# Last two expert groups summed expert by expert, and another order of the first loads, in a decoder layer with 32 experts

## The chip, the cores and the metric

One Trainium2 chip, one of its cores. The metric is the device time of one execution in microseconds (us), the median of three runs.

## The reference

One decoder layer on 256 tokens of width 1024, in float32. The part that the change touches is the input projection of the attention and the mixture of experts.

```
h    = rms_norm(x) * norm1_g                      # 256 x 1024
proj = h @ w_in                                   # 1024 x 3072: q, k, v of two head groups
...                                               # attention of both groups, output projection, x = x + ...
t    = rms_norm(x) * norm2_g
g    = argmax(t @ router_group)                   # 1 of 4 groups
e    = top 2 of the group's 8 experts             # weights: p_group * softmax of the two
y[token] += weight * ((silu(t @ w_gate[e]) * (t @ w_up[e])) @ w_down[e])
out  = x + y                                      # hidden width of an expert: 256, 32 experts
```

## The kernel before, in words

**Weights.** All weights pass through SBUF in units of 1 MB: 12 of `w_in`, 4 of `w_out`, then gate, up and down of the 32 experts, in the order in which they are used (gate e, up e, down e−2). A ring of 16 buffers and a few more tiles hold them; `fill` (L120) issues every load on SyncE's queue (SP) as soon as the list `used` says that the buffer's earlier unit is consumed in program order, and the transfer itself waits on the chip until the reader is done. `unit` (L145) calls it.

**Start.** TensorE warms up on zeros (`keep_warm`, L161). x comes twice: transposed (`xt`, into qT and kT, which are free at that time) for the projection, and in rows (x2, L406) for the residual and for the scale of the RMS norm. `x_split` (L197) makes of each 128-wide slice k of the transposed x a rounded half `xh` (ScalarE) and a remainder `xl` (VectorE); `stage` (L239) does the same with 128 rows of a weight unit (`hi` on ScalarE, `lo` on VectorE, two of them on POOL). Four buffers of each are in rotation. A product is then three matmuls (xh·hi, xl·hi, xh·lo), for each of the two token halves c. The projection runs over six column groups ng of 512 columns (q, k, v, twice), each with eight slices k, two to a step b. The two accumulators of a group (`pps`) are both PSUM buffers of their tag, so the next group begins when they are copied out by `post_qk` (L264). That copy multiplies with `rstd`, which `x_norm` (L205) makes from x2 by two squares with a sum (L209), a logarithm and an exponential (L153, L154) and some small VectorE work.

**Experts.** Eight groups g of four experts, 32 slots each. `prep` (L607) makes a group's selection matrices Pm and Ps and gathers its tokens (L615). Per expert: `gate` (L662), `folded` of the expert before (L672), `up` (L668), and `down` (L696) of the one before that; the loop is at L881. A group's results gather in `oG`, 32 rows an expert, by four copies an expert (L707, L709); `weighted` (L633) makes the weighted, transposed selection pT, and `combine` (L723) adds the whole group to the four accumulators y with 8 matmuls (16 instructions) two experts later. The last group goes another way: `weighted_last` (L620) makes a pT for each of its experts with the selection repeated four times, at expert 30; `down` leaves its result in the four row blocks of one 128 x 256 tile, two copies (`moved`, L711); and `spread` (L715) adds one expert with 8 matmuls (16 instructions) on 32 rows each. `residual` (L731) adds x through the identity. `last` (L736) does the second half of expert 31's down product in two halves of the columns, each with its copy, its spread, and its stores. `overflow` (L755), after expert 28, is a branch that all engines take part in; it is not taken with these inputs.

The order of each engine's instructions is made when the program is built, by a scheduler that works with priorities; in the expert loop `pe` (L647) keeps TensorE in program order.

Of the kernel before, what the change touches and what calls it, by code (L numbers as in the profile page):

```python
# [20 lines left out]
P = 128  # L21
S = 256
# [29 lines left out]
def hybrid_layer_kernel(ctx: ExitStack, tc: tile.TileContext, x, xt, w_in, w_out, w_gate, w_up, w_down, smalls, relb, out):  # L52
# [49 lines left out]
    units[0] = (*units[0][:2], 2)  # L102
# [17 lines left out]
    def fill(i, limit=len(units)):  # L120
        while len(tiles) < limit:
# [49 lines left out]
    with ExitStack() as att:  # L171
# [67 lines left out]
        def stage(u, k):  # L239
# [4 lines left out]
            (nc.gpsimd if u * 4 + k in (0,3,) else nc.vector).tensor_tensor(lo, raw, hi.bitcast(F32), op=ALU.subtract)  # L244
# [195 lines left out]
        for ng, what in enumerate("qkvqkv"):  # L440
            g = ng // 3
            pps = new_pp()
            for b in range(4):
# [7 lines left out]
                for c in range(NC):  # L451
                    products(hl, c, b * 2, b == 0, b == 3, pps[c])
# [137 lines left out]
    CROSS = [(j, c) for c in range(NC) for j in range(4)]  # L590
# [29 lines left out]
    def weighted_last(st):  # L620
        t = pools["late"].tile([P, 2048], F32, name="oL", tag="late")
        st["o"], st["pT"] = t[:, :D].rearrange("p (i n) -> p i n", i=G), t[:, D:].rearrange("p (i t) -> p i t", i=G)
        for i in range(G):
            pt = ps.tile([P, 512], F32, name="ptr", tag="tr")
            for c in range(NC):
                q = st["P"][c][1].rearrange("p (j s) -> p j s", j=G)
                e = st["g"] * G + i
                nc.vector.tensor_scalar(q, st["P"][c][0][:, i : i + 1, :].broadcast_to([P, G, CAP]),
                                        W[:, c, e : e + 1], None, op0=ALU.mult)
                pe(nc.tensor.transpose(pt[:, c * P : (c + 1) * P], q.rearrange("p j s -> p (j s)"), ident))  # L630
            nc.scalar.activation(st["pT"][:, i, :], pt[:, :S], AF.Copy)

    def weighted(st):  # L633
        g = st["g"]
        if g == E // G - 1:
            return weighted_last(st)
# [59 lines left out]
    def down(e, st, hT, low):  # L696
# [4 lines left out]
        if st["g"] == E // G - 1:  # L701
            moved(st, i, pd, slice(0, P))
            return
# [7 lines left out]
    def moved(st, i, pd, rows):  # L711
# [277 lines left out]
```

## Time and profile before

| what | value |
|---|---|
| median of 3 runs | 344.23 us (343.37 to 344.47) |
| the profiled execution: its time, its span | 344.96 us, 343.2 us |
| TensorE busy, share of the span | 314.5 us, 92% |
| VectorE, ScalarE, POOL busy | 194.3, 139.9, 17.3 us |
| read from HBM | 121.64 MB, 358 GB/s over the span |

The span is shorter than the time of the execution by what lies around the first and the last instruction. Busy time of TensorE holds matmuls that wait in its pipeline, so a busy fortieth doesn't say that it runs at its peak; what waits for what is in the views below. DMA issues stand as "SPq" and "ACTq", weight loads as "PEld".

### The profile page before, as it was taken

Reading aid. Unit: us, or ns where it says so; the run is one execution under the profiler, and the core shown is the slowest. Engines: PE = TensorE matmul, PEld = TensorE weight load, DVE = VectorE, ACT = ScalarE, POOL = GpSimd, SP = SyncE. Lnnn points to the kernel's source line nnn. Section 1 sums busy time; section 2 is a strip of 40 time slices with the busy share of each in tenths; the row PEclk is TensorE's granted clock in tenths of the full one; section 3 lists DMA queues with packets and bytes.
Section 4 is the critical chain, followed back from the end, with each engine's and each line's share of the span. In section 5 each row is a group of like instructions: output and inputs, shape, how many; then the busy total and the mean of one; then the engine's idle time right before and its main releaser. Section 6 shows DMA issues by size and latency. Waiting matters only on the chain. (4 is left out here: it accounts for less than half of the span.)

```text
span 343.2 us, 7327 instructions
## 1 busy us (share of the span) xinstructions
PE 314.5 (92%) x2801; PEld 217.4 (63%) x2801; DVE 194.3 (57%) x599; ACT 139.9 (41%) x364; POOL 17.3 (5%) x25
## 2 busy tenths in 40 slices
PE   6999999999999999999999999998489669968893
PEld 2758877788777797576666766566257326625461
DVE  1867858869998658665463654736224522532502
ACT  4876667968886443423232232321112211211302
POOL 1100001000110140000000000000000000040000
PEclk9899999999999999999999999999989978989997
DMA  6999999999635888899999999999999999999903
GB/s 197 403 385 317 389 387 402 413 411 409 209 99 210 319 355 320 303 423 418 416 416 415 415 421 418 413 421 413 416 418 416 418 415 420 416 411 420 362 10 122
DMA packets 29496, 123.20 MB, mean 359 GB/s; under 512 B 2295, under 2 KB 3364, under 8 KB 21268
## 3 DMA queue, kind: packets, MB, share of 16 engines
q1 hardware_dynamic: 28868, 121.17, 89.1%
q0 software_dynamic: 304, 1.02, 1.0%
q8 instruction: 23, 0.38, 0.4%
q10 hardware_dynamic: 288, 0.52, 0.4%
q14 instruction: 13, 0.11, 0.1%
HBM read 121.64 MB, written 1.07 MB: 358 GB/s over the span
## 5 line engine op out<-in xcount | busy, mean ns | idle before, releaser
L658 PE MATMUL pgu<-u,xe 128*32 128x256 f32 x976 | 67.4, 395 | 10.1 <-ACT oG L707 4.8
L254 PE MATMUL pp<-hi,xh 128*128 128x512 f32 (+1 forms) x132 | 53.3, 405 | 2.6 <-ACT hi L243 2.6
L254 PE MATMUL pp<-lo,xh 128*128 128x512 f32 (+1 forms) x132 | 52.1, 399 | 0.3 <-POOL lo L244 0.2
L254 PE MATMUL pp<-hi,xl 128*128 128x512 f32 (+1 forms) x132 | 51.9, 393 | 0.0
L707 ACT ACTIVATE oG<-pd 32x256 f32<-32x256 f32 x56 | 21.0, 374 | 75.0 <-PE pd L693 61.4
L658 PEld LDWEIGHTS pgu<-u,xe 128*32 128x32 f32 x976 | 29.5, 111 | 34.6 <-ACT oG L707 8.6
L244 DVE TENSOR_TENSOR lo<-u,hi 128x512 fp32r<-128x512 f32 x62 | 43.1, 714 | 13.0 <-ACT hi L243 12.7
L243 ACT ACTIVATE hi<-u 128x512 fp32r<-128x512 f32 x64 | 38.9, 626 | 18.3 <-PE pp L254 12.6
L709 DVE COPY oG<-pd 32x256 f32<-32x256 f32 x56 | 23.7, 423 | 38.7 <-ACT oG L707 36.8
L693 PE MATMUL pd<-u,hT 128*32 128x256 f32 x496 | 34.9, 394 | 6.6 <-DMA u<-in_w_down_dram 6.6
L254 PEld LDWEIGHTS pp<-hi,xh 128*128 128x128 f32 x132 | 25.1, 190 | 9.6 <-ACT hi L243 4.0
L254 PEld LDWEIGHTS pp<-lo,xh 128*128 128x128 f32 x132 | 25.3, 192 | 7.4 <-issue 1.0
L254 PEld LDWEIGHTS pp<-hi,xl 128*128 128x128 f32 x132 | 25.2, 191 | 4.6
L670 DVE COPY u<-pgu 128x256 f32<-128x256 f32 x30 | 12.7, 422 | 26.7 <-PE pgu L658 23.6
L615 PEld LDWEIGHTS pg<-Ps,x2q 128*128 128x128 f32 x224 | 25.5, 192 | 2.9 <-DVE gu L678 2.9
L693 PEld LDWEIGHTS pd<-u,hT 128*32 128x32 f32 x496 | 14.5, 112 | 20.0 <-DVE u L670 7.5
L615 PE MATMUL pg<-Ps,x2q 128*128 128x128 f32 x224 | 26.9, 278 | 0.0
L728 PE MATMUL y<-oG,pT 128*128 128x256 f32 x112 | 26.4, 391 | 0.0
L728 PEld LDWEIGHTS y<-oG,pT 128*128 128x128 f32 x112 | 21.8, 200 | 2.8
L678 DVE TENSOR_REDUCE gu<-ptr 128x64 f32<-128x256 f32 x32 | 13.6, 425 | 14.5 <-PE ptr L675 13.8
L675 PEld LDWEIGHTS ptr<-sm,u 128*128 128x128 f32 x120 | 13.4, 147 | 13.1 <-issue 9.9
L675 PE MATMUL ptr<-sm,u 128*128 128x128 f32 x120 | 21.0, 301 | 0.0
(166 smaller groups left out, 342.0 us busy)
## 6 DMA issues: line engine op xcount, KB each, us to landing
u<-in_w_up_dram SPq DMA_DIRECT2D x31, 1024.0 KB, 19.9
u<-in_w_gate_dram SPq DMA_DIRECT2D x30, 1024.0 KB, 19.9
u<-in_w_down_dram SPq DMA_DIRECT2D x30, 1024.0 KB, 19.9
u<-in_w_in_dram SPq DMA_DIRECT2D x11, 1024.0 KB, 12.0
u<-in_w_out_dram SPq DMA_DIRECT2D x4, 1024.0 KB, 14.6
x<-in_w_gate_dram SPq DMA_DIRECT2D x2, 1024.0 KB, 9.0
u<-in_w_in_dram SPq DMA_DIRECT2D x2, 512.0 KB, 6.0
x<-in_x_dram SPq DMA_DIRECT2D x2, 512.0 KB, 10.9
```

Of the source, the lines that this page charges most:

```text
L243: nc.scalar.activation(hi, raw, AF.Copy)
L244: (nc.gpsimd if u * 4 + k in (0,3,) else nc.vector).tensor_tensor(lo, raw, hi.bitcast(F32), op=ALU.subtract)
L254: yield lambda a=a, w=w, kk=kk, i=i: nc.tensor.matmul(pp, a, w[:, cols], start=first and kk == 0 and i == 0, stop=last and kk == len(hls) ...
L615: pe(nc.tensor.matmul(pg[:, j * P : (j + 1) * P], x2q[:, c, q4 * 4 + j, :], st["P"][c][1], start=c == 0, stop=c == NC - 1))
L658: pe(nc.tensor.matmul(pg[q * CAP : (q + 1) * CAP, :HID], st["xe"][:, k, j0 : j0 + CAP], wv[:, k, :], start=r == 0, stop=r == KC // ROWS_Q ...
L670: nc.vector.tensor_copy(t[:, HID : 2 * HID], pg[:, :HID])
L675: pe(nc.tensor.transpose(pt[:, j * P : (j + 1) * P], t[:, j * P : (j + 1) * P], ident))
L678: nc.vector.tensor_reduce(gu[:, :2], parts[:, :2], axis=AX.X, op=ALU.add)
L693: pe(nc.tensor.matmul(pd[j * 32 : (j + 1) * 32, :256], hT[:, c, :], dv[:, c, j * 256 : (j + 1) * 256], start=c == 0, stop=c == 1, tile_pos ...
L707: nc.scalar.activation(dst, pd[j * 32 : (j + 1) * 32, :256], AF.Copy)
L709: nc.vector.tensor_copy(dst, pd[j * 32 : (j + 1) * 32, :256])
L728: pe(nc.tensor.matmul(y[j][:, c * 256 : c * 256 + 256], st["pT"][:, c * P : (c + 1) * P], st["o"][:, j * 256 : (j + 1) * 256], start=st["g ...
```

## The change

- The groups 6 and 7 (`APART` is 6) are both summed expert by expert. `weighted_last` is split: `repeated` writes the repeated selection on VectorE, `weighted_last` transposes it and copies it out. For group 6 one expert at a time (24 to 27), for group 7 the experts 28 and 29 at expert 28's turn, 30 and 31 at expert 29's. Every expert's `spread` stands one expert behind its `down`. `combine` is left out for group 6.
- The tiles for these two groups and the copy of x (`res`) take buffers of the ring (`spare`); the copy of x on POOL stands at expert 28, and the residual is added in two pieces, at expert 30 and after 31.
- The last expert's second half goes in one wave: 8 matmul instructions, two copies, one spread, eight copies out, four stores.
- At the start, unit 0 comes in three parts: slice 0 and slice 1 on ScalarE's queue, slices 2 and 3 on SP's. The first slices of the transposed x go ahead on SP, unit 2 goes ahead of x in rows. The table of the activation functions is loaded behind ScalarE's two issues. One of the two remainders on POOL goes to VectorE.
- In the first column group the matmuls run slice by slice with both token halves in each slice, where it was step by step with one half after the other.

```diff
-    nc.scalar.preload_act_table_set("natural_log_exp_and_others")
     head = A_COLS["gq"][0]
-    nc.sync.dma_start(sm[:, :head], smalls[:, :head])
...
-    units[0] = (*units[0][:2], 2)
+    units[0] = (*units[0][:2], 3)
...
                 if j == 0:
-                    ks = slice(q * k // parts, (q + 1) * k // parts)
-                    nc.sync.dma_start(tv[:, ks], src[:, ks])
-                    xt_load(2, 4) if q == 0 else xt_load(4, 8)
+                    ks = slice(*((0, 1), (1, 2), (2, 4))[q])
+                    (nc.sync if q == 2 else nc.scalar).dma_start(tv[:, ks], src[:, ks])
+                    if q == 2:
+                        xt_load(4, 8)
...
-            (nc.gpsimd if u * 4 + k in (0,3,) else nc.vector).tensor_tensor(lo, raw, hi.bitcast(F32), op=ALU.subtract)
+            (nc.gpsimd if u * 4 + k == 3 else nc.vector).tensor_tensor(lo, raw, hi.bitcast(F32), op=ALU.subtract)
...
         keep_warm(11, "av")
+        nc.sync.dma_start(sm[:, :head], smalls[:, :head])
         xt_load(0, 2)
+        xt_load(2, 4)
         unit(0)
+        nc.scalar.preload_act_table_set("natural_log_exp_and_others")
+        early["units"] = 3
+        fill(0, 3)
         for c in range(NC):
             nc.sync.dma_start(x2[:, c, :], x[c * P : (c + 1) * P, :])
...
-                for c in range(NC):
-                    products(hl, c, b * 2, b == 0, b == 3, pps[c])
+                if ng == 0:
+                    for kk in range(2):
+                        for c in range(NC):
+                            products(hl[kk : kk + 1], c, b * 2 + kk, b + kk == 0, b + kk == 4, pps[c])
+                else:
+                    for c in range(NC):
+                        products(hl, c, b * 2, b == 0, b == 3, pps[c])
...
+    APART = E // G - 2
+    def spare(name):
+        used["ring"].append(len(units))
+        return ring.tile([P, 2048], F32, name=name, tag="ring")
+    def last_group(st):
+        t = spare("oL")
...
+    def repeated(st, i):
+        e = st["g"] * G + i
+        for c in range(NC):
+            q = st["P"][c][1].rearrange("p (j s) -> p j s", j=G)
+            nc.vector.tensor_scalar(q, st["P"][c][0][:, i : i + 1, :].broadcast_to([P, G, CAP]),
+                                    W[:, c, e : e + 1], None, op0=ALU.mult)
+    def weighted_last(st, i):
+        pt = ps.tile([P, 512], F32, name="ptr", tag="tr")
+        for c in range(NC):
+            pe(nc.tensor.transpose(pt[:, c * P : (c + 1) * P], st["P"][c][1], ident))
+        nc.scalar.activation(st["pT"][:, i, :], pt[:, :S], AF.Copy)
...
-        if st["g"] == E // G - 1:
-            moved(st, i, pd, slice(0, P))
+        if st["g"] >= APART:
+            moved(st, i, pd)
...
+    def last(st, hT, dv, pd, res):
         for nh in range(2):
             down_product(hT, dv, pd, (1,), (2 * nh, 2 * nh + 1))
+        moved(st, G - 1, pd)
+        spread(st, G - 1)
+        for c in range(NC):
+            for j in range(4):
+                dst = res[:, c, j * 256 : (j + 1) * 256]
+                if j < 2:
+                    nc.scalar.activation(dst, y[j][:, c * 256 : c * 256 + 256], AF.Copy)
+                else:
+                    nc.vector.tensor_copy(dst, y[j][:, c * 256 : c * 256 + 256])
+            for nh, eng in enumerate((nc.scalar, nc.sync)):
...
         if i == 0:
             before, st = old, nxt
+            if g >= APART:
+                last_group(st)
         t = gate(e, st)
         queue.append((e - 1, old, folded(old_t)))
-        if i == 2 and g > 0:
+        apart = () if g < APART else (i,) if g == APART else ((0, 1), (2, 3), (), ())[i]
+        if apart:
+            repeated(st, apart[0])
+        if i == 2 and 0 < g <= APART:
             combine(before)
         up(e, st, t)
+        for k, j in enumerate(apart):
+            if k:
+                repeated(st, j)
+            weighted_last(st, j)
...
+        if done:
+            spread(*done.pop())
         if e == E - 1:
             hT = folded(t)
         if e > 1:
-            down(*queue.pop(0), place[e][0])
+            e2, st2, hT2 = queue.pop(0)
+            down(e2, st2, hT2, place[e][0])
+            if st2["g"] >= APART:
+                done.append((st2, e2 % G))
         if e == OVER_E:
             overflow()
-        if e == E - 1:
-            rt_ = ring.tile([P, 2048], F32, name="res", tag="ring")
-            res = rt_.rearrange("p (c n) -> p c n", c=NC)
+            res = spare("res").rearrange("p (c n) -> p c n", c=NC)
...
+        if e == E - 2:
+            residual(0, res)
+    residual(1, res)
     down(*queue.pop(0), place[E - 1][0])
...
+    spread(*done.pop())
+    dv = unit(place[E - 1][2]).rearrange("p (c n) -> p c n", c=2)
+    pd = ps.tile([P, 512], F32, name="pd", tag="tr")
+    down_product(hT, dv, pd, (0,), range(4))
+    spread(st, 2)
+    warmed(2, "pp")
+    last(st, hT, dv, pd, res)
```

What the scheduler makes of it, at three places. ScalarE behind the halves of unit 1 (u_124), before: the two squares of x (sq,ss) and the scale's logarithms and exponentials (ry) stand ahead of every half (hi) of unit 2 (u_129).

```order
L243 ACTIVATE hi<-u_124 128x512 x4
L209 ACTIVATE sq,ss<-x_64 128x1024 x2
L153 ACTIVATE ry<-rv 128x1
L154 ACTIVATE ry<-ry 128x1
L153 ACTIVATE ry<-rv 128x1
L154 ACTIVATE ry<-ry 128x1
L270 ACTIVATE qk<-pp,rstd 128x512
L276 ACTIVATE sq<-qk 128x512
L243 ACTIVATE hi<-u_129 128x512 x2
```

The same place in the changed kernel (unit 2 is u_127 there):

```order
L242 ACTIVATE hi<-u_124 128x512 x4
L242 ACTIVATE hi<-u_127 128x512 x3
L208 ACTIVATE sq,ss<-x_64 128x1024
L242 ACTIVATE hi<-u_127 128x512
L152 ACTIVATE ry<-rv 128x1
L208 ACTIVATE sq,ss<-x_64 128x1024
L153 ACTIVATE ry<-ry 128x1
L152 ACTIVATE ry<-rv 128x1
L153 ACTIVATE ry<-ry 128x1
L269 ACTIVATE qk<-pp,rstd 128x512
```

All four halves of unit 2 moved ahead of the end of the scale's chain, the fourth to between the two squares.

TensorE from expert 30's gate to expert 28's down, before: behind the fold (ptr<-sm,u) the sum of group 6 (y<-oG,pT), behind the up product eight weighted transposes (ptr<-sm,Ps).

```order
L658 MATMUL pgu<-u_3100,xe 32x256 x8
L675 MATMUL ptr<-sm,u_3042 128x128 x4
L728 MATMUL y<-oG,pT 128x256 x8
L658 MATMUL pgu<-u_3102,xe 32x256 x8
L630 MATMUL ptr<-sm,Ps 128x128 x8
L693 MATMUL pd<-u_3177,hT 32x256 x8
```

The same in the changed kernel:

```order
L673 MATMUL pgu<-u_3101,xe 32x256 x8
L690 MATMUL ptr<-sm,u_3043 128x128 x4
L673 MATMUL pgu<-u_3103,xe 32x256 x8
L733 MATMUL y<-oL 128x256 x8
L708 MATMUL pd<-u_3181,hT 32x256 x8
L748 MATMUL y<-res,sm 128x256 x4
```

The group's sum and the transposes went out; a spread of one expert (27) and half of the residual came in.

TensorE from expert 30's down product to the end, before (pd<-u_3282 is expert 31's):

```order
L693 MATMUL pd<-u_3280,hT 32x256 x8
L733 MATMUL y<-res,sm 128x256 x8
L718 MATMUL y<-oL 128x256 x8
L693 MATMUL pd<-u_3282,hT 32x256 x4
L688 LDWEIGHTS zeros
L688 MATMUL warm<-zeros 128x512
L688 LDWEIGHTS zeros
L688 MATMUL warm<-zeros 128x512
L693 MATMUL pd<-u_3282,hT 32x256 x2
L718 MATMUL y<-oL 128x256 x4
L693 MATMUL pd<-u_3282,hT 32x256 x2
L718 MATMUL y<-oL 128x256 x4
```

The same in the changed kernel (expert 31's is pd<-u_3346):

```order
L708 MATMUL pd<-u_3296,hT 32x256 x8
L733 MATMUL y<-oL 128x256 x8
L708 MATMUL pd<-u_3346,hT 32x256 x4
L733 MATMUL y<-oL 128x256 x8
L703 LDWEIGHTS zeros
L703 MATMUL warm<-zeros 128x512
L703 LDWEIGHTS zeros
L703 MATMUL warm<-zeros 128x512
L708 MATMUL pd<-u_3346,hT 32x256 x4
L733 MATMUL y<-oL 128x256 x8
```

The residual stands ahead of these rows now, and the last expert's two halves are one.

## Rows read from the trace of the kernel before

**Rows 1.** The page, its first line and the row of its second part that gives the memory traffic in 40 equal slices of the span (8.58 us each), in GB/s.

```profile
span 343.2 us, 7327 instructions
GB/s 197 403 385 317 389 387 402 413 411 409 209 99 210 319 355 320 303 423 418 416 416 415 415 421 418 413 421 413 416 418 416 418 415 420 416 411 420 362 10 122
```

**Rows 2.** Who the queue SP waited for before it could issue a load, from 137 to 150 us (first row) and from 180 to 240 us (second): line waited at, releaser, us in total, times, longest.

```profile
SPq L138 <- PE pl L875: 7.9, 1, 7.9
...
SPq L138 <- DMA u<-in_w_gate_dram: 16.5, 8, 2.2
```

**Rows 3.** Who TensorE waited for, from 0 to 150 us; the same columns.

```profile
PE pp L254 <- ACT hi L243: 2.6, 2, 1.9
...
PE pp L856 <- DVE gi L546: 0.5, 1, 0.5
```

**Rows 4.** The timeline of the start: start in us, busy us, engine, line, operation, out<-in, how many; in brackets the idle time before it and what ended that.

```profile
7.47 0.50 PE L254 MATMUL pp<-hi,xh 128*128 128x512 f32 x1 [1.90 <-ACT hi L243]
...
7.50 1.29 POOL L244 TENSOR_TENSOR lo<-u,hi 128x512 fp32r<-128x512 f32 x1 [7.05 <-ACT hi L243]
...
13.63 2.19 ACT L243 ACTIVATE hi<-u 128x512 fp32r<-128x512 f32 x4 [1.04 <-DMA u<-in_w_in_dram]
...
15.02 0.40 PE L254 MATMUL pp<-hi,xh 128*128 128x512 f32 x1
...
15.73 1.04 ACT L209 ACTIVATE sq<-x 128x1024 f32<-128x1024 f32 x1
...
16.89 1.06 ACT L209 ACTIVATE sq<-x 128x1024 f32<-128x1024 f32 x1
...
18.00 0.39 PE L254 MATMUL pp<-hi,xl 128*128 128x512 f32 x1
...
18.32 0.81 PE L226 MATMUL pb<-rb 33*12 33x384 f32 x2
...
18.50 0.20 ACT L154 ACTIVATE ry<-ry 128x1 f32<-128x1 f32 x1
...
20.45 0.69 ACT L270 ACTIVATE qk<-pp,rstd 128x512 f32<-128x512 f32 x1 [1.74 <-DVE rstd L159]
...
22.37 0.50 PE L254 MATMUL pp<-hi,xh 128*128 128x512 f32 x1 [0.75 <-ACT hi L243]
```

**Rows 5.** Busy time in four stretches: stretch in us, its length, then busy us (and instructions) of PE, PEld, DVE, ACT, POOL, the clock granted to TensorE (1.00 is its upper level, 0.50 the lower), the share of the DMA engines, GB/s.

```profile
2.00:5.00 3.00, 3.00 (x9) 1.06 (x7) 0.00 (x0) 0.03 (x1) 0.00 (x0) 1.00 0.66 169
...
8.80:12.00 3.20, 3.15 (x8) 2.51 (x9) 2.60 (x5) 2.65 (x6) 1.18 (x1) 0.50 1.03 406
...
306.40:308.70 2.30, 2.28 (x21) 0.83 (x24) 1.31 (x4) 0.26 (x1) 2.22 (x3) 0.50 1.02 406
308.70:320.00 11.30, 9.15 (x84) 5.89 (x80) 3.77 (x13) 2.78 (x8) 0.00 (x0) 0.99 1.01 415
```

**Rows 6.** The timeline of the experts 27 to 30, columns as in rows 4.

```profile
289.23 1.07 PE L693 MATMUL pd<-u,hT 128*32 128x256 f32 x16
...
289.33 0.47 DVE L599 TENSOR_SCALAR Ps<-Pm,rstd 128x128 f32<-128x128 f32 x2
...
292.68 3.50 PE L615 MATMUL pg<-Ps,x2q 128*128 128x128 f32 x29
...
300.89 1.07 PE L693 MATMUL pd<-u,hT 128*32 128x256 f32 x16 [0.93 <-DMA u<-in_w_down_dram]
...
303.28 0.43 DVE L709 COPY oG<-pd 32x256 f32<-32x256 f32 x1 [0.44 <-ACT oG L707]
...
304.42 1.07 PE L658 MATMUL pgu<-u,xe 128*32 128x256 f32 x16 [2.46 <-DVEq L758]
...
310.86 1.07 PE L658 MATMUL pgu<-u,xe 128*32 128x256 f32 x16 [1.17 <-DMA u<-in_w_gate_dram]
```

**Rows 7.** The issue of expert 31's up weights on SP (columns as in rows 4), the page's row for such loads (KB each, median us from issue to landing), and the memory traffic around the last data (columns as in rows 5).

```profile
300.77 0.33 SPq L138 DMA_DIRECT2D u<-in_w_up_dram  x1
...
u<-in_w_up_dram SPq DMA_DIRECT2D x31, 1024.0 KB, 19.9
...
327.00:328.00 1.00, 1.00 (x20) 0.42 (x16) 0.00 (x0) 0.00 (x0) 0.00 (x0) 1.00 0.11 33
```

**Rows 8.** The timeline of the end, from the sum of group 6 on, columns as in rows 4.

```profile
312.36 3.62 PE L728 MATMUL y<-oG,pT 128*128 128x256 f32 x16
...
316.91 0.44 PE L630 MATMUL ptr<-sm,Ps 128*128 128x128 f32 x2
...
319.65 1.07 PE L693 MATMUL pd<-u,hT 128*32 128x256 f32 x16
...
325.09 2.01 PE L718 MATMUL y<-oL 32*128 32x256 f32 x32
...
333.87 0.62 PE L693 MATMUL pd<-u,hT 128*32 128x256 f32 x4
...
334.54 0.27 ACT L712 ACTIVATE oL<-pd 64x128 f32<-64x128 f32 x1 [6.09 <-PE pd L693]
...
337.74 1.13 PE L718 MATMUL y<-oL 32*128 32x256 f32 x8 [0.87 <-DVE oL L713]
...
338.94 0.76 DVE L752 COPY res<-y 128x256 f32<-128x256 f32 x2 [1.26 <-PE y L718]
...
339.45 0.34 ACTq L753 DMA_DIRECT2D out_dram<-res  x1
```

More of the change, by code (lines that the diff above doesn't have):

```diff
@@ L589, in hybrid_layer_kernel @@
     x2n = x2q.rearrange("t c k p -> t c p k")
-    CROSS = [(j, c) for c in range(NC) for j in range(4)]
+    APART = E // G - 2
     g2p = A_COLS["g2p"][0]
@@ L709, in down, with moved, spread @@
                 nc.vector.tensor_copy(dst, pd[j * 32 : (j + 1) * 32, :256])
-    def moved(st, i, pd, rows):
-        nc.scalar.activation(st["o"][rows, i, :P], pd[rows, :P], AF.Copy)
-        nc.vector.tensor_copy(st["o"][rows, i, P:], pd[rows, P:256])
-    def spread(st, i, pairs):
-        for j, c in pairs:
+    def moved(st, i, pd):
+        nc.scalar.activation(st["o"][:, i, :P], pd[:, :P], AF.Copy)
+        nc.vector.tensor_copy(st["o"][:, i, P:], pd[:, P:256])
+    def spread(st, i):
+        for c, j in [(c, j) for c in range(NC) for j in range(4)]:
             r = slice(j * CAP, (j + 1) * CAP)
             pe(nc.tensor.matmul(y[j][:, c * 256 : c * 256 + 256], st["pT"][r, i, c * P : (c + 1) * P],
-                                st["o"][r, i, :], start=False, stop=i == G - 1 and c == NC - 1, tile_position=(j * CAP, 0)))
+                                st["o"][r, i, :], start=False, stop=st["g"] == E // G - 1 and i == G - 1 and c == NC - 1, tile_position=(j * CAP, 0)))
     y = []
@@ L734, in residual @@
                                 start=False, stop=False))
-    def last(e, st, hT, res):
-        dv = unit(place[e][2]).rearrange("p (c n) -> p c n", c=2)
-        pd = ps.tile([P, 512], F32, name="pd", tag="tr")
-        down_product(hT, dv, pd, (0,), range(4))
-        warmed(2, "pp")
+    def last(st, hT, dv, pd, res):
         for nh in range(2):
             down_product(hT, dv, pd, (1,), (2 * nh, 2 * nh + 1))
-            moved(st, G - 1, pd, slice(nh * 64, nh * 64 + 64))
-            j0 = 2 * nh
-            spread(st, G - 1, [(j, c) for c in range(NC) for j in (j0, j0 + 1)])
-            for c, eng in enumerate((nc.scalar, nc.sync)):
-                for j in (j0, j0 + 1):
-                    dst = res[:, c, j * 256 : (j + 1) * 256]
-                    if j == j0:
-                        nc.scalar.activation(dst, y[j][:, c * 256 : c * 256 + 256], AF.Copy)
-                    else:
-                        nc.vector.tensor_copy(dst, y[j][:, c * 256 : c * 256 + 256])
+        moved(st, G - 1, pd)
[8 more added lines that the diff above has]
+            for nh, eng in enumerate((nc.scalar, nc.sync)):
                 eng.dma_start(out[c * P : (c + 1) * P, nh * 512 : nh * 512 + 512], res[:, c, nh * 512 : nh * 512 + 512])
@@ L879, in hybrid_layer_kernel @@
         nc.vector.tensor_copy(flag, cm)
-    before, queue = None, []
+    before, queue, done = None, [], []
     for e in range(1, E):
@@ L907, in hybrid_layer_kernel @@
                                           x2n[:, c, nh * 64 : (nh + 1) * 64, :])
-    spread(st, 0, CROSS)
-    spread(st, 1, CROSS)
+        if e == E - 2:
+            residual(0, res)
+    residual(1, res)
     down(*queue.pop(0), place[E - 1][0])
-    residual(0, res)
-    residual(1, res)
-    spread(st, 2, CROSS)
-    last(E - 1, st, hT, res)
+    spread(*done.pop())
[5 more added lines that the diff above has]
+    last(st, hT, dv, pd, res)
 _OUTS = [((1, 256, 1024), "float32")]
```

15 lines of the change are left out of this document (1 added, 14 removed).

## The prediction

> **What bounds the kernel now.** I read the page first: its fortieths say that the stream of weights is short of its 415 GB/s only at the start, from 86 to 146 us, and after 317 us [rows 1]. Two engines could hold the stream back in the middle, and the queue's own waits tell which: until 150 us SP waits for TensorE to give buffers back, from 180 us for earlier transfers [rows 2]. So whatever delays or advances TensorE before 150 us shifts the whole stream behind it, one to one. TensorE's own waits are short: in the first 150 us 2.6 us for the first halves of the weights, all before 22.4 us, and after that 0.5 us [rows 3]. TensorE thus bounds the first 150 us and passes any stall at 22 us on to the end.
>
> The end is different. From expert 30's gate on (310.86 us) no matmul waits for a transfer: the last up weights, issued at 300.77 us, land 19.9 us later, at 320.7, the last down weights stop moving data at about 328 us [rows 7], yet the last expert's second half begins at 333.87 us [rows 8]. TensorE's own list is the bound there, 28 us of it, and work taken out of it counts in full until TensorE meets those landings.
>
> **The end, part by part**, behind expert 30's gate. (1) The 16 instructions (from 312.36) that sum group 6 leave: −3.6 us [rows 8]. (2) The eight weighted transposes with their ping-pong to VectorE leave: 316.91 to 319.65, −2.7 us. (3) Expert 27's spread now stands here: half of the 2.01 us that two took, +1.0. The residual stays, in two pieces. (4) The last expert in one wave: today its two halves take 333.87 to 337.74 until the last spread starts, 3.9 us; now 8 instructions, about 0.7, and two moves of 0.27 with their gaps, 0.65: −2.5. That spread has 16 instructions instead of 8, and the copies behind it are two pairs on either engine instead of one (0.76 a pair), the first beside the spread: +0.2 if the clock is full, +0.9 if halved, I take +0.5. ScalarE issues both its stores behind its copies: +0.35 for the second (0.34 today). Together −1.65 (−1.9 to −0.65). Sum behind the gate: −6.95.
>
> What went out stands earlier, where TensorE had slack. Expert 27: transposes 0.4, a wait of some 0.8 since VectorE may write the next group's selection only after them (two operations of 0.25 behind the copy of up), a spread 1.0; experts 28 and 29: two pairs of transposes (half of 2.7) and a spread, 2.4 each. That is 7.0 us. Their cover, today's gaps between 292.68 and 310.86 [rows 6]: 0.93 before 300.89; at the branch TensorE waits until four small copies are done in turn (some 0.42 each, the last from 303.28 to 303.71), and two moves of 0.27 are 1.1 us shorter; gate 29 to gate 30 takes 6.44 us where four such blocks elsewhere take 3.45 (289.23 to 292.68), 3.0. Cover 5.0, so gate 30 comes 2.0 us later. But 1.2 us of the cover is a stretch at half clock (306.40 to 308.70, granted 0.50) behind the 2.46 us gap at the branch [rows 5, 6]; that gap shrinks to some 1.4. The 0.75 us gap before 22.37 was followed by none, the 1.9 us before 7.47 by one of 3.2 us. In between, I count a quarter of it: 2.3 us. **End: −4.65 us**, from −5.8 (a few waits of 0.2 gone too, full clock) to −2.75. TensorE then reaches the last up weights at 320.7 to 321, just as they land, so a cheaper list would gain little more. The new tiles in the ring take buffers whose reader (expert 25 at the latest) finished some 20 us before the transfers that now use them are issued; I cost them at nothing.
>
> **The start.** Before, the first matmul runs at 7.47 us, the fifth slice of the contraction at 15.02, and the second column group starts at 22.37 [rows 4]. Three things move.
> (a) The first matmul needs a quarter of unit 0 instead of a half, from a second queue. In 2 to 5 us the 16 engines were busy 0.66 of the time at 169 GB/s [rows 5]: a second queue could fill at most the idle third, 1.0 us, or nothing; I take 0.5. Before, 836 KB had to land first (68 + 256 + 512); with the queues sharing evenly, it is twice 68 + 256, 648 KB, 0.3 us less. So 0.8 us earlier, and with the same 7.55 us for four slices the fifth starts at 14.2. Unit 1 allows no more than 13.2 to 14.2: it landed at 13.63, its bytes are the same, and a first half costs 0.55. −0.8 (−1.8 to −0.5).
> The Trainium skill (DMA: Bandwidth & Descriptors, section "Issuing engines are not separate DMA queues") says that transfers started by several engines run on the same 16 engines and save no more than issue time; by it the 0.5 would be 0 and the sum 342.2 us. That rule speaks against this edit; the idle third above leaves it open, and no row here has two queues loading.
> (b) The two squares of x were done by 18.0 us, in ScalarE's idle time beside the matmuls, and the scale waited for nobody. Now unit 2's first halves stand ahead of them in ScalarE's order: three before the first square, the fourth between the two. The fourth can't start before the 48th matmul has read the buffer that it reuses. Behind the end of those matmuls come therefore 0.15 for the signal, 0.55 for the half, 0.2 for a logarithm, 1.81 from the second square's start to its last exponential (16.89 to 18.70), 0.2 for the other exponential, 0.7 for the copy that frees the accumulator: 3.6 us, in which TensorE has only the bias matmul (0.74). From the fifth slice to the second group it was 7.35 us; now 24 matmuls at 0.23 (13 steps from 15.02 to 18.00) and 3.6, 9.1. **+1.75**. Only the order costs: x was there at 15.73 and comes one unit later, 2.7 us at some 390 GB/s, 18.4; the first square can start at about 18.7, the second at 20.7.
> (c) That leaves TensorE idle for 2.9 us. Both longer gaps above were followed by half clock, for 3.2 and 2.3 us, so it loses half of such a stretch: +1.2, from 0 to 1.6.
> The first remainder moved from POOL (1.29 us) to VectorE and the table load moved behind two issues on ScalarE are hidden by the first landing; if they weren't, 0.4 us.
> **Start: +2.15 us**, from 0 to +3.3; nothing later waits, so nothing is given back.
>
> **Sum**: −4.65 + 2.15 = −2.5 us. The profiled execution took 344.96 us (span 343.2, 1.76 around it), 0.73 above the median of 344.23. Against that median: 341.7 us.
>
> **The rivals.**
> *The start costs nothing* (0.18). Two queues fill the idle third, unit 1 lands 1 us earlier, and the clock holds through the gap. For it: the low rates of the first 5 us. Against: the two half-clock stretches. Then −4.65 + 0: 339.6 us. The rule cited above would give it no chance; the engines' idle third gives it some.
> *The clock falls twice* (0.14): behind the scale's stall and again behind the branch, the last spread at half clock too. End −2.75, start +2.5 to +3.3: between −0.25 and +0.55, 344.0 to 344.8, no change that shows.
> *Slower* (0.08): TensorE runs experts 29 to 31 largely at half clock, because the three blocks of small work ahead of them, with VectorE between the transposes, are too loose to keep it up. Full-clock work costs as much again at half clock. From the forecast, 2.5 us of it bring the time back to where it was and 3.5 us make it measurably slower; a third of the 22 us of work behind gate 29, 7 us, gives 348.7. For it: 0.50 in 306.40 to 308.70. Against: 0.99 in 308.70 to 320 with the same small work.
> *The edit does not do what it says* (0.02): x was in row order before too, only its place in the queue is new; a sum by expert that landed in the same place would leave the end as it is. In the changed order the spreads and transposes do stand earlier. 346.4 us then, the start's cost alone.
>
> **How the numbers follow.** The forecast has 0.58, 340.2 to 343.2 by itself. About 0.3%, 1.0 us, is what a measurement of this kernel can tell from no change. Faster by more: the forecast without its upper edge, 0.56, and the first rival, 0.18, together 0.74; within: that edge, 0.02, and the second rival, 0.14, together 0.16; slower: 0.08 and 0.02, 0.10. Range: down to 338.6 (end −5.8, start +0.2), up to 344.0, where the second rival begins.
>
> **What would show it.** At the start: first matmul at 6.5 to 7.2 us, the second column group at 23.5 to 24.5, just before it a wait of TensorE of about 3 us for ScalarE, and half clock behind it. At the end: no 16-instruction sum behind gate 30, gate 30 at 1.5 to 4 us later against the stream, the last expert's second half about 5 us earlier against the last landing, one wave of eight copies. The prediction is wrong if the squares of x run before the 48th matmul ends, if the stream waits for a buffer after 290 us, or if TensorE waits for landings between gates 29 and 31.

## The result and the profile after

The changed kernel took 341.6 us (340.79 to 342.92, 9 runs) beside 343.71 us (342.78 to 344.81, 9 runs) for the kernel before: ratio 0.9939 (0.9919 to 0.9959), **2.1 us faster**. Measured a second time, beside the experiments: 341.68 to 343.91 us, 0.9940 (0.9915 to 0.9965). Its profiled execution took 341.6 us, span 339.8; that of before lies 1.25 us above its median of 343.71, so the two profiles differ by 3.4 us where the medians differ by 2.1. The forecast was a change of −2.5 us.

The start, from the timeline of the changed kernel, answers to [rows 4]:

```profile
6.95 1.04 PE L253 MATMUL pp<-hi,xh 128*128 128x512 f32 x2 [2.05 <-ACT xh L200]
...
14.19 0.40 PE L253 MATMUL pp<-hi,xh 128*128 128x512 f32 x1
...
18.82 1.05 ACT L208 ACTIVATE sq<-x 128x1024 f32<-128x1024 f32 x1
...
20.47 1.04 ACT L208 ACTIVATE sq<-x 128x1024 f32<-128x1024 f32 x1
...
22.50 0.69 ACT L269 ACTIVATE qk<-pp,rstd 128x512 f32<-128x512 f32 x1
...
23.24 0.50 PE L253 MATMUL pp<-hi,xh 128*128 128x512 f32 x1 [2.67 <-ACT qk L269]
...
33.22 1.03 PE L288 MATMUL pt<-sm,qk 128*128 128x128 f32 x8
```

The last row, the first transposes of q and k, in the kernel before:

```profile
31.17 1.03 PE L289 MATMUL pt<-sm,qk 128*128 128x128 f32 x8
```

From the fifth slice to the second column group it is now 9.05 us (before 7.35), and TensorE waits 2.67 us for ScalarE's copy. At the first transposes TensorE is 2.05 us late. The stretches (columns as in [rows 5]) show two more things: more bytes in the first 5 us, and the lower clock level (0.50, called half clock here) behind that wait.

```profile
2.00:5.00 3.00, 2.90 (x10) 0.90 (x7) 0.47 (x1) 1.58 (x2) 0.00 (x0) 1.00 0.84 231
...
24.00:26.00 2.00, 2.00 (x7) 1.53 (x6) 1.44 (x3) 0.60 (x1) 0.00 (x0) 0.56 1.03 391
26.00:28.00 2.00, 2.00 (x7) 1.59 (x6) 0.69 (x1) 1.22 (x3) 0.00 (x0) 0.59 1.08 349
```

The end, from the issue of expert 31's up weights on; it answers to [rows 6 to 8]:

```profile
301.29 0.47 SPq L137 DMA_DIRECT2D u<-in_w_up_dram  x1
...
306.11 1.07 PE L673 MATMUL pgu<-u,xe 128*32 128x256 f32 x16 [1.37 <-DVEq L769]
306.30 4.16 POOL L929 COPY res<-x2q 128x512 f32<-128x512 f32 x4 [173.96 <-DMA u<-in_w_up_dram]
...
308.67 0.88 DVE L697 TENSOR_TENSOR hT<-gu 128x64 f32<-128x64 f32 x1
...
309.81 0.94 DVE L641 TENSOR_SCALAR Ps<-Pm,W 128x128 f32<-128x128 f32 x2
310.60 0.52 PE L647 MATMUL ptr<-sm,Ps 128*128 128x128 f32 x2 [1.46 <-DVE Ps L641]
...
313.02 1.05 PE L673 MATMUL pgu<-u,xe 128*32 128x256 f32 x16
...
321.36 1.07 PE L673 MATMUL pgu<-u,xe 128*32 128x256 f32 x16
...
331.20 0.64 PE L708 MATMUL pd<-u,hT 128*32 128x256 f32 x8
...
332.56 1.15 PE L733 MATMUL y<-oL 32*128 32x256 f32 x16 [0.72 <-DVE oL L728]
333.79 1.21 ACT L760 ACTIVATE res<-y 128x256 f32<-128x256 f32 x4 [1.60 <-PE y L733]
333.88 1.42 DVE L762 COPY res<-y 128x256 f32<-128x256 f32 x4 [1.37 <-PE y L733]
334.75 0.84 ACTq L764 DMA_DIRECT2D out_dram<-res  x2
335.04 0.85 SPq L764 DMA_DIRECT2D out_dram<-res  x2
```

Read it in three pieces. The last up weights are issued 0.52 us later than before. Gate 30 (313.02) comes 11.73 us behind that issue, before 10.09: +1.64. From gate 30 to the last expert's second half it is 18.18 us, before 23.01: −4.83. From there to the end of the span it is 8.6 us, before 9.33: −0.73. Together −3.4, the difference of the spans. And the up weights, issued at 301.29 and 19.9 us under way, are used at 321.36, 20.07 us later: TensorE now meets them as they land.

### The profile page after: what moved, and what is told of

Its sections match the earlier page's. It is cut to its first block, busy times and chain, and to the rows that moved or that the text cites. A ratio compares the mean times of both kernels' runs of the same rounds, so it can differ in the third digit from the quotient of the medians.

```text
span 339.8 us, 7433 instructions
## 1 busy us (share of the span) xinstructions
PE 311.0 (92%) x2855; PEld 215.6 (63%) x2855; DVE 195.0 (57%) x601; ACT 138.7 (41%) x362; POOL 16.1 (5%) x24
## 3 DMA queue, kind: packets, MB, share of 16 engines
q0 software_dynamic: 304, 1.02, 1.0%
## 5 line engine op out<-in xcount | busy, mean ns | idle before, releaser
L673 PE MATMUL pgu<-u,xe 128*32 128x256 f32 x976 | 65.7, 387 | 8.9 <-ACT oG L722 4.2
L243 DVE TENSOR_TENSOR lo<-u,hi 128x512 fp32r<-128x512 f32 x63 | 43.3, 702 | 19.9 <-ACT hi L242 19.3
L253 PE MATMUL pp<-hi,xl 128*128 128x512 f32 (+1 forms) x132 | 52.9, 401 | 0.0
L722 ACT ACTIVATE oG<-pd 32x256 f32<-32x256 f32 x48 | 17.9, 374 | 60.2 <-PE pd L708 48.5
L724 DVE COPY oG<-pd 32x256 f32<-32x256 f32 x48 | 20.3, 423 | 30.7 <-ACT oG L722 29.0
L708 PE MATMUL pd<-u,hT 128*32 128x256 f32 x496 | 33.2, 383 | 3.3 <-DMA u<-in_w_down_dram 3.3
L743 PE MATMUL y<-oG,pT 128*128 128x256 f32 x96 | 21.7, 379 | 0.0
L690 PE MATMUL ptr<-sm,u 128*128 128x128 f32 x120 | 20.1, 291 | 0.0
L743 PEld LDWEIGHTS y<-oG,pT 128*128 128x128 f32 x96 | 17.8, 190 | 2.2
## 6 DMA issues: line engine op xcount, KB each, us to landing
u<-in_w_up_dram SPq DMA_DIRECT2D x31, 1024.0 KB, 19.9
x<-in_w_down_dram SPq DMA_DIRECT2D x1, 1024.0 KB, 19.9
```

The costliest lines, as they stand in the source:

```text
L243: (nc.gpsimd if u * 4 + k == 3 else nc.vector).tensor_tensor(lo, raw, hi.bitcast(F32), op=ALU.subtract)
L253: yield lambda a=a, w=w, kk=kk, i=i: nc.tensor.matmul(pp, a, w[:, cols], start=first and kk == 0 and i == 0, stop=last and kk == len(hls) ...
L673: pe(nc.tensor.matmul(pg[q * CAP : (q + 1) * CAP, :HID], st["xe"][:, k, j0 : j0 + CAP], wv[:, k, :], start=r == 0, stop=r == KC // ROWS_Q ...
L690: pe(nc.tensor.transpose(pt[:, j * P : (j + 1) * P], t[:, j * P : (j + 1) * P], ident))
L708: pe(nc.tensor.matmul(pd[j * 32 : (j + 1) * 32, :256], hT[:, c, :], dv[:, c, j * 256 : (j + 1) * 256], start=c == 0, stop=c == 1, tile_pos ...
L722: nc.scalar.activation(dst, pd[j * 32 : (j + 1) * 32, :256], AF.Copy)
```

## The experiments

The kernel before was timed in each set beside the others; "against before" is the ratio times 344 us.

| kernel | median, us | ratio (95% interval) | against before, us |
|---|---|---|---|
| start's edits alone | 345.9 | 1.0047 (1.0016 to 1.0078) | +1.6 |
| end's edits alone | 340.54 | 0.9892 (0.9856 to 0.9928) | −3.7 |
| changed, x ahead of unit 2 again | 338.31 | 0.9816 (0.9779 to 0.9854) | −6.3 |
| changed, x copied by ScalarE in a row | 344.02 | 0.9981 (0.9954 to 1.0008) | −0.7 |
| before, TensorE delayed by 5 us | 349.28 | 1.0159 (1.0139 to 1.0180) | +5.5 |
| changed, its wait at 20 us filled | 341.77 | 0.9948 (0.9928 to 0.9967) | −1.8 |
| x ahead, ScalarE's copies spread | 338.46 | 0.9849 (0.9825 to 0.9873) | −5.2 |
| changed, squares ahead in ScalarE's order | 339.78 | 0.9866 (0.9843 to 0.9890) | −4.6 |
| two queues alone, x ahead | 342.34 | 0.9950 (0.9933 to 0.9967) | −1.7 |

**The two halves of the change, each alone on the kernel before.** The start's edits (queues, slice order, x behind unit 2), then the end's (spread by expert, last expert in one wave):

```diff
...
+        early["units"] = 3
+        fill(0, 3)
         for c in range(NC):
             nc.sync.dma_start(x2[:, c, :], x[c * P : (c + 1) * P, :])
...
```

> The start's edits alone, on the kernel before. Both theories: the second column group starts 0.9 us later (23.2 us), then half clock, and TensorE is 2.1 us late from 30 to 150 us. Theory A (as predicted, one to one): the whole stream and the end are 2.1 us late, 345.8 us against 343.7. Theory B (the slowest of the DMA engines are never without work after 115 us, so they, and with them the landings, lose only what exceeds their backlog): the last up weights land 0.5 us later, 344.2 us.

```diff
...
-    CROSS = [(j, c) for c in range(NC) for j in range(4)]
+    APART = E // G - 2
...
```

> The end's edits alone, on the kernel before. Theory A: the change's 341.6 us minus the start's 2.1 us, 339.5 us. Theory B: minus 0.5 us, 341.1 us; the last up weights land as before (320.7 us in the profile) and the span ends about 18.5 us behind that.

Start +1.6, end −3.7, sum −2.1: the change's own time. The start is a loss inside a change that gains. The start alone came out as theory A has it (345.9 for 345.8 us), but its interval, +0.6 to +2.7 us, almost reaches theory B's +0.5; the pure delay below decides. The end alone, 340.54 us, lies between A's 339.5 and B's 341.1. In the profile of the end alone, the 1.47 us wait ahead of the last transposes was followed by the lower clock (0.63 on average over 3 us); in the changed kernel's profile 1.46 us at the same place was not. Of the six profiles with a wait of 1.44 to 1.47 us there, two show the lower clock behind it: this one and that with the squares ahead.

```profile
309.40:312.40 3.00, 3.00 (x33) 1.51 (x36) 0.00 (x0) 0.38 (x1) 0.00 (x0) 0.63 1.03 425
```

**x in rows ahead of unit 2 again**, all else as changed:

```diff
-        early["units"] = 3
-        fill(0, 3)
         for c in range(NC):
             nc.sync.dma_start(x2[:, c, :], x[c * P : (c + 1) * P, :])
+        early["units"] = 3
+        fill(0, 3)
```

> The changed kernel with x in rows ahead of unit 2 again, as before; two queues and slice order kept. Both theories: the squares of x run beside the matmuls, the wait of 2.7 us and the half clock behind it go, the second column group starts at 21.5 us (23.24 in the change, 22.37 before), and TensorE is 0.8 us ahead of the kernel before until 150 us. Theory A: 2.9 us faster than the change, 338.7 us. Theory B: the landings come no earlier than before, 0.5 us faster than the change, 341.1 us.

338.31 us, the best of all kernels here, and near theory A's 338.7. The second column group starts at 21.30 us instead of 23.24, the last up weights are issued 2.9 us earlier:

```profile
21.30 0.50 PE L253 MATMUL pp<-hi,xh 128*128 128x512 f32 x1 [0.54 <-ACT hi L242]
...
298.38 0.33 SPq L137 DMA_DIRECT2D u<-in_w_up_dram  x1
```

So the delay of TensorE at 20 us is passed on to the last load, not absorbed.

**A pure delay of TensorE**, 23 matmuls on zeros in the middle of the second column group of the kernel before:

```diff
+                if ng == 1 and b == 2:
+                    t = ps.tile([P, 512], F32, name="warm", tag="av")
+                    for _ in range(23):
+                        with tc.issue_after(state["mm"].ins):
+                            state["mm"] = nc.tensor.matmul(t, zeros, zeros.unsqueeze(1).broadcast_to([P, 4, P]), start=True, stop=True)
```

> The kernel before with 23 matmuls on zeros (about 5.0 us) in TensorE's row in the middle of the second column group, which delay it without idle time. Theory A (whatever delays TensorE before 150 us shifts the whole weight stream one to one): issue of the last expert's up matrix at 305.5 to 306, 349.1 us, ratio 1.0145. Rival B (some 1.6 us of a delay are taken up by slack in the stream): issue at 304 to 304.4, 347.5 us, ratio 1.010.

```profile
306.19 0.33 SPq L138 DMA_DIRECT2D u<-in_w_up_dram  x1
```

+5.5 us for 5.0 inserted; the last up weights were issued at 306.19 us (before 300.77, +5.42), and this profile's second group had already started 1.0 us later than before. One to one within 0.5 us; theory B (issue at 304 to 304.4 us) falls.

**What x's late place costs: its landing or ScalarE's order?**

```diff
...
-                nc.scalar.activation(sq, x2[:, c, :], AF.Square, accum_out=ss)
+                state["sq"] = nc.scalar.activation(sq, x2[:, c, :], AF.Square, accum_out=ss)
...
-            nc.scalar.activation(hi, raw, AF.Copy)
+            if (u, k) == (2, 2):
+                with tc.issue_after(state["sq"].ins):
+                    nc.scalar.activation(hi, raw, AF.Copy)
+            else:
+                nc.scalar.activation(hi, raw, AF.Copy)
...
```

> The changed kernel with one edit: the third half of unit 2 is split on ScalarE behind both squares of x, not ahead of them; the loads stay as changed (x behind the third weight unit). Theory O (what x's place costs lies in ScalarE's order, as the forecast had it: the squares could start when the second half of unit 2 is done, at 17.6 us): squares at 17.6 and 18.8, second column group at 21.5 to 22.2 instead of 23.2, TensorE's wait for the copy out of PSUM 1.0 to 1.7 us instead of 2.67, no half clock behind it, 340.0 us (ratio 0.989). Rival L (x is not there sooner: its landing sets the squares): first square no earlier than 18.3 us, second group at 22.8 or later, 341.5 us (0.993).

```profile
16.86 1.05 ACT L208 ACTIVATE sq<-x 128x1024 f32<-128x1024 f32 x1
...
18.56 1.04 ACT L208 ACTIVATE sq<-x 128x1024 f32<-128x1024 f32 x1
...
20.32 0.51 PE L257 MATMUL pp<-hi,xh 128*128 128x512 f32 x1 [0.35 <-ACT qk L273]
...
298.06 0.56 SPq L137 DMA_DIRECT2D u<-in_w_up_dram  x1
...
320.04 1.07 PE L677 MATMUL pgu<-u,xe 128*32 128x256 f32 x16
```

The same loads, one edge in ScalarE's order: the first square runs 2 us earlier, the second group 2.9 us (2.4 to 2.5 against the two profiles whose first group ran at full clock as this one's did), the wait is 0.35 us, the clock stays at 1.00 to 30 us, and 1.9 us of median time come back (2.5 by the ratios). x had been there by 16.86 us: most of the cost was the order, not the landing, as theory O has it. Not all: unit 2's last halves now stand behind the squares, and the first transposes start at 29.91 us, 1.1 us later than with x ahead (28.82 in the profile of the two queues alone, whose first group ran at full clock too). Nor does all of the gain reach the end: the last up weights were issued 3.2 us earlier than in the changed kernel, but the 1.46 us wait ahead of the last transposes was followed by the lower clock in this profile (0.50 in 310 to 312 us), and TensorE came to them 22.0 us after their issue instead of 20.1.

**The wait at 20 us filled**, so that TensorE does not idle:

```diff
+                if ng == 1 and b == 0:
+                    t = ps.tile([P, 512], F32, name="warm", tag="av")
+                    for _ in range(11):
+                        with tc.issue_after(state["mm"].ins):
+                            state["mm"] = nc.tensor.matmul(t, zeros, zeros.unsqueeze(1).broadcast_to([P, 4, P]), start=True, stop=True)
```

> The changed kernel with 11 matmuls on zeros (about 2.4 us) behind the first column group, so that TensorE is not idle while the second group waits for ScalarE's copy out of PSUM; the order of ScalarE and the place of x stay as changed. Theory A (the wait of 2.67 us is what brings the half clock behind it, and every us that TensorE loses before 150 us comes out at the end): the second column group still starts at 23.0 to 23.4 us, the granted clock stays at 1.0 from 22 to 28 us, where the changed kernel's rows have 0.56 and 0.59 (2.0 x 0.44 + 2.0 x 0.41 = 1.7 us lost), and the time is 1.7 us below the changed kernel's: 340.0, 0.989 of the kernel before. Rival C (the half clock there doesn't hang on that wait): clock still near 0.5 in 24 to 28, 341.6 us, ratio 0.994. Rival B (the stretch is full speed but the stream of weights sets the end): 341.3.

> The changed kernel once more, beside the others on one chip, so that their differences to it are taken from the same runs: 341.6 us, 0.994 of the kernel before; second column group at 23.2, wait of 2.67 us, clock 0.55 to 0.6 from 24 to 28 us; wait for VectorE ahead of gate 30 of 1.46 us.

The stretch behind the wait, with the fill, and then in the second profile of the changed kernel:

```profile
24.00:26.00 2.00, 2.00 (x11) 1.59 (x10) 1.24 (x4) 0.93 (x4) 0.00 (x0) 1.00 1.00 377
26.00:28.00 2.00, 2.00 (x10) 1.64 (x9) 1.92 (x9) 0.70 (x2) 0.00 (x0) 1.00 0.93 204
```

```profile
24.00:26.00 2.00, 1.17 (x3) 0.97 (x4) 1.86 (x7) 1.70 (x4) 0.00 (x0) 0.50 0.48 104
26.00:28.00 2.00, 2.00 (x7) 1.52 (x6) 1.04 (x3) 0.21 (x1) 0.00 (x0) 0.50 1.05 398
28.00:30.00 2.00, 2.00 (x6) 1.61 (x5) 0.69 (x1) 0.81 (x3) 0.00 (x0) 0.50 0.96 284
```

So the lower clock does hang on that wait, but filling it saved no median time (341.77 to 341.68), and theory A's 340.0 us is a miss. The fill has a price of its own: fifth slice to second group 9.60 us, in two profiles of the start's edits with a first group at full clock 9.16 and 9.20. From the second group to the first transposes of q and k it takes 8.45 us with the fill, 9.98 without it in three profiles, and 11.02 in the second profile of the changed kernel, whose single execution took 345.5 us: the half clock costs TensorE 1.5 us or more there, of which the fill takes 0.4 back. The last up weights are issued at 300.30 us with the fill, and at 300.73 to 301.31 in the three profiles. What the half clock costs on average stays open: nothing by the medians, about 1.5 us by the rows.

**Two queues alone**: the start's edits with x ahead of unit 2, the end as before (the first fence's edit undone).

> The kernel before with the start's edits but x left ahead of the third weight unit: two queues for the first loads and the two k of each half pair taken one by one, the end as before. The forecast's own term: 0.8 us less, 343.1 (ratio 0.9977). By the marks of the third experiment (second column group at 20.8 to 21.3 us where the kernel before has 22.4): 1.2 us less, 342.7 (0.9965). By the difference of the third to the second experiment's times: 2.2 us less, 341.7 (0.9935).

The first 5 us, the fifth slice, and TensorE around the bias matmul (L225); then the same three rows of TensorE where the start is the kernel before's, in the profile of the end's edits alone:

```profile
2.00:5.00 3.00, 3.00 (x9) 1.06 (x7) 0.41 (x1) 1.58 (x2) 0.00 (x0) 1.00 0.88 260
...
13.28 0.50 PE L253 MATMUL pp<-hi,xh 128*128 128x512 f32 x1 [0.71 <-ACT hi L242]
...
18.95 0.81 PE L225 MATMUL pb<-rb 33*12 33x384 f32 x2
20.30 0.50 PE L253 MATMUL pp<-hi,xh 128*128 128x512 f32 x1 [0.54 <-ACT hi L242]
```

```profile
14.29 0.50 PE L254 MATMUL pp<-hi,xh 128*128 128x512 f32 x1 [0.25 <-ACT hi L243]
...
17.69 0.81 PE L226 MATMUL pb<-rb 33*12 33x384 f32 x2
...
21.75 0.50 PE L254 MATMUL pp<-hi,xh 128*128 128x512 f32 x1 [0.75 <-ACT hi L243]
```

−1.7 us (−2.3 to −1.1). Both profiles run the first group at full clock. The fifth slice starts at 13.28 against 14.29 us, and from there to the second group it takes 7.02 against 7.46: the bias matmul now stands in the wait behind the group, where it used to split the group. Within the second group 0.26 us more are gained: from its start to the first transposes it takes 8.52 us (20.30 to 28.82), before 8.78 (21.75 to 30.53). Together 1.7 us.

**The copies of x on ScalarE**, first in a row, then one by one (the second on the kernel with x ahead of unit 2):

```diff
...
-                    nc.gpsimd.tensor_copy(res[:, c, nh * 512 : (nh + 1) * 512].rearrange("t (p k) -> t p k", k=KC),
-                                          x2n[:, c, nh * 64 : (nh + 1) * 64, :])
+                    nc.scalar.activation(res[:, c, nh * 512 : (nh + 1) * 512].rearrange("t (p k) -> t p k", k=KC),
+                                         x2n[:, c, nh * 64 : (nh + 1) * 64, :], AF.Copy)
...
```

> The changed kernel with the four copies of x for the residual on ScalarE instead of POOL. Both theories: VectorE's selections (0.94 us for two) and the product hT (0.88) at expert 29 fall back to 0.47 and 0.23, TensorE's wait of 1.46 us at 310.6 goes, and gate 30 starts 1.0 to 1.4 us earlier. Theory C (TensorE's own list bounds the end, as predicted): 1.0 us faster, 340.6 us. Theory D (the last up weights' landing bounds it, TensorE reaches them only 0.07 us after they land): 0.1 us faster, 341.5 us, and a wait of about 1 us for that landing appears.

```profile
305.49 4.10 ACT L929 ACTIVATE res<-x2q 128x512 f32<-128x512 f32 x4 [1.01 <-DVEq L769]
...
310.05 0.23 DVE L697 TENSOR_TENSOR hT<-gu 128x64 f32<-128x64 f32 x1 [1.40 <-ACT gu L694]
310.19 0.48 DVE L641 TENSOR_SCALAR Ps<-Pm,W 128x128 f32<-128x128 f32 x2
310.52 0.60 PE L647 MATMUL ptr<-sm,Ps 128*128 128x128 f32 x2 [2.00 <-DVE Ps L641]
```

Both expectations missed. VectorE is at its usual pace again, but the four copies stand in a row ahead of ScalarE's own part of the chain (L694), so TensorE waits 2.00 us instead of 1.46, the clock falls behind it, and gate 29 to gate 30 takes 9.0 us instead of 6.9. The second form takes the copies into ScalarE's gaps:

```diff
...
+    def res_copy(c, nh):
+        with tc.issue_after(state["act"].ins):
+            return nc.scalar.activation(res[:, c, nh * 512 : (nh + 1) * 512].rearrange("t (p k) -> t p k", k=KC),
+                                        x2n[:, c, nh * 64 : (nh + 1) * 64, :], AF.Copy)
...
+            if e == OVER_E + 1:
+                res_copy(0, k)
...
+        if e == E - 2:
+            copy10 = res_copy(1, 0)
+            copy11 = res_copy(1, 1)
...
```

> The changed kernel with x loaded ahead of the third weight unit again (as in the third experiment, 338.3 us), and with the four copies of x into the residual's tile on ScalarE instead of GpSimd, one behind each of two weighted copies of expert 29 and two behind the copy-out of expert 29's product, in ScalarE's gaps. Theory V (VectorE's operations between two SBUF tiles take longer beside GpSimd's copy, 0.88 for 0.23 us and 0.94 for 0.48 us, and that is most of the 1.46 us that TensorE waits ahead of the last weighted transposes): that wait falls to 0.3 to 0.5 us, gate 29 to gate 30 from 6.9 to 5.8 us, 337.2 us, ratio 0.979. Rival W (the wait comes from the chain reduce, Silu, product, scaling as it is): wait 1.3 to 1.5, 338.3 us, ratio 0.982. Rival S (ScalarE's copies hold up its other work as they did in a row of four): wait of 1 us or more for ScalarE at another place, 339.3, ratio 0.985.

```profile
298.24 0.33 SPq L137 DMA_DIRECT2D u<-in_w_up_dram  x1
...
305.61 0.23 DVE L697 TENSOR_TENSOR hT<-gu 128x64 f32<-128x64 f32 x1
...
306.13 0.47 DVE L641 TENSOR_SCALAR Ps<-Pm,W 128x128 f32<-128x128 f32 x2
...
306.46 0.52 PE L647 MATMUL ptr<-sm,Ps 128*128 128x128 f32 x2 [0.37 <-DVE Ps L641]
...
308.88 1.05 PE L673 MATMUL pgu<-u,xe 128*32 128x256 f32 x16
...
318.22 1.07 PE L673 MATMUL pgu<-u,xe 128*32 128x256 f32 x16 [0.35 <-SPq L769]
```

Theory V has its mechanism: wait 0.37 us, gate 29 to gate 30 5.8 us. Its time is a miss: 338.46 us against 338.31 (timed in different sets; −5.2 and −6.3 by the ratios). TensorE is 1.1 us earlier and gives it back, in waits of 0.17, 0.46 and 0.35 us on the next three pieces of weights, and begins the last up product at 318.22, 20 us after its issue. Besides, 2.1 to 2.4 us of each execution of the two kernels with copies on ScalarE lie around the span, where it is 1.8 in the changed kernel; no run shows why. From that product to the end of the span it is 18.4 us in this profile, in the changed kernel's and in that with x ahead. The landing of the last up weights sets the end there. From their issue to the end of the span it is 42.3 to 42.6 us in the four profiles with the end as before; 38.4 to 38.5 in the five with the new end in which TensorE meets the landing; and 40.3 to 40.6 in the three (end alone, squares ahead, copies in a row) whose clock fell behind the wait ahead of the last transposes: there TensorE came 22 us after the issue and its own list was the bound.

## Why the prediction was right, point by point

The forecast was 341.7 us, measured were 341.6 and 341.68. That it fits to 0.1 us is partly luck: the kernel before came out 0.52 us lower in nine runs (343.71) than in the three that the forecast stands on (344.23), and the change was −2.1 us, not −2.5. The mechanisms were those forecast; the start's terms came as reckoned, some of the end's did not, and they partly cancel.

- **One to one.** "Whatever delays or advances TensorE before 150 us shifts the whole stream behind it": held, by the pure delay (+5.5 for 5.0) and by x's place (2.9 us of issue). Over all twelve profiles the first transposes of q and k start anywhere from 28.8 to 35.9 us, and from there to the issue of the last up weights it is 268.1 to 269.6 us in each (less the 5.0 inserted where it was). So a single profile can hide or add up to 1.5 us on the way: the changed kernel's 2.05 us of delay are 0.52 at that issue against the profile of before, and 2.15 against that of the end alone.
- **Start (a), −0.8.** Hit: the fifth slice came at 14.19 us, 0.83 earlier, and at full clock 1.0 earlier (13.28 for 14.29). The first matmul came at 6.95 us; in all nine profiles with two queues it waits for the transposed x (xh), no longer for the weights. The second queue did fill idle time of the engines: 228 to 260 GB/s in 2 to 5 us at a busy share of 0.84 to 0.90 in these nine, 158 to 175 at 0.65 to 0.79 in the three with one queue; on average 75 GB/s more, 0.2 MB in 3 us. The rule of the Trainium skill (DMA: Bandwidth & Descriptors, section "Issuing engines are not separate DMA queues") grants issue time alone. The trace agrees, and shows what that is worth where the issues of one queue leave the engines partly idle: the first part of unit 0 is issued at 0.74 us instead of 1.66. The two queues alone gained 1.7 us, though: behind the fifth slice 0.7 more, most of it the bias matmul, which the new order hides in the wait. The forecast has no term for it; in the changed kernel it goes under in the stall of (b).
- **Start (b), +1.75.** Hit: 9.05 less 7.35 us, 1.70, and the order of ScalarE shown as most of its cause. The first square could have started at 16.86, though, not 18.7: x had landed by then. One sign of being wrong came by the letter: the first square (18.82) ran before the 48th matmul ended (it began at 19.44). The reckoning itself has it there; the second square, which sets the scale, ran behind (20.47).
- **Start (c), +1.2.** Hit: the half clock came in all four profiles with the 2.67 us wait. From the second group to the first transposes it is 9.98 us, before 8.80, +1.18; with the changed start and no half clock 8.45 to 8.53 in four profiles, so the half clock costs 1.5. Sum of the start by these rows: −0.83 + 1.70 + 1.18 = +2.05, forecast +2.15; by the medians +1.6 (0.6 to 2.7). x's late place alone costs more than that, 3.3 us by the start's two forms (+1.6 and −1.7), since it also loses the 0.7 above.
- **End, gate 30.** +2.3 forecast against the stream, +1.64 measured: the gap at the branch shrank to 1.37 us and no half clock followed. In the two profiles with the lower clock behind the next wait gate 30 came 13.26 and 13.56 us after the issue, +3.2 and +3.5 (end alone, squares ahead); the forecast's 2.3 lies between. Inside the +1.64 is a loss not forecast: VectorE's hT takes 0.88 us for 0.23 and its two Ps 0.94 for 0.47 beside GpSimd's copy of x, and TensorE waits 1.46 us.
- **End, behind gate 30.** Removals (1) to (3) were to give −5.3 until the last expert's second half; −4.83 came: the residual in two pieces takes 0.19 us more (twice 1.92 for 3.65), and TensorE waits 0.2 us for the last up weights (0.78 us from the fold to the product, without a wait 0.58). The last expert's second half comes 3.2 us earlier against the last landing, about what these terms give (2.3 − 5.3), not the "about 5 us" named among the signs. "TensorE then reaches the last up weights just as they land, so a cheaper list would gain little more" is what the spread copies showed.
- **End, last wave, −1.65.** Mis-sized: −0.73. Its terms reach from −1.95 to −1.25; the upper edge of −0.65 does not follow from them. The wave itself gave −2.5 as said (331.20 to 332.56, where before it was 3.87 us). The copies behind the last spread's start took 0.78 us more (forecast 0.5). The stores cost +1.0, not +0.35: from the end of the copies to the end of the span it is 4.5 us (335.30 to 339.8), before 3.5 (339.70 to 343.2). Four stores now go together, two issues on either queue, and each lands later. The page's list of issues has for the kernel before, then for the changed one:

```profile
out_dram<-res ACTq DMA_DIRECT2D x2, 256.0 KB, 2.1
out_dram<-res SPq DMA_DIRECT2D x2, 256.0 KB, 2.4
```

```profile
out_dram<-res ACTq DMA_DIRECT2D x2, 256.0 KB, 2.5
out_dram<-res SPq DMA_DIRECT2D x2, 256.0 KB, 2.9
```

- **The sum.** End −3.7 for −4.65 and start +1.6 for +2.15: a miss of 0.95 one way and 0.55 the other, both within the intervals (end −5.0 to −2.5, start +0.6 to +2.7). By the rows the end gave −3.9 (+1.64 − 4.83 − 0.73), and the last wave is its largest miss. The rival "the start costs nothing" falls. "The clock falls twice" was in neither of the two profiles of the changed kernel; the fall at the end was in two of the six profiles with this end.

## What to carry to other kernels

When a transfer is moved later in a queue, look at what its reader then stands behind in its engine's order: here the data was there, and one edge in ScalarE's order gave back most of the loss. A delay ahead of a saturated stream arrived at its end in full here (5.5 us for 5.0), while work taken out behind the last landing's issue counts only until the compute meets that landing. Price a last wave by its stores too: merging removed steps worth 2.5 us, but the stores that then go together took 1.0 us more where nothing hides them.

## What the runs showed of the hardware

- GpSimd's copy between SBUF tiles (four of 1.04 us) held up VectorE's operations between SBUF tiles, 0.23 to 0.88 us and 0.47 to 0.94, while those that read PSUM beside it kept 0.41 to 0.42 us. On ScalarE the same copies took 1.02 to 1.12 us each and left VectorE at 0.23 and 0.47 to 0.48. The Trainium skill (SBUF — State Buffer, section "SBUF: two separate sides") says that VectorE and GpSimd share a pair of ports which, for some forms of VectorE's instructions, one of them holds for a whole instruction. The trace agrees: hT ends at 309.55, just behind the end of the third copy (309.4 by an estimate, three quarters of the row at 306.30).
- At one place, ahead of the last transposes, an idle time of TensorE of 1.44 to 1.47 us was followed by the lower clock level in two of six profiles; 2.67 us at 20 us was followed by it in four of four, 1.36 to 1.37 us at the branch in none of eight. The first column group ran at 0.50 for a stretch in some profiles of every start and at 1.00 in others, worth about 0.7 us at the fifth slice (15.02 and 14.29 us with the same start). Single profiles of this kernel differ by that much for no reason in the code.
